# The last down pair of an MLP: kept product sums read back by plain transfers, and a second group of seven products

## The chip, the cores and the metric

The kernel runs on one core of one Trainium2 chip. The metric is the device time of one execution in microseconds, the median of repeated runs. Engine names are those of the profile: PE (matmul) with its weight loads PEld, DVE (vector), ACT (scalar), POOL (gpsimd), SP (the queue that issues most transfers).

## The reference

A decoder trunk of two layers on 256 tokens with 2048 features, in float32. Layer 0 has a dilated-window attention, layer 1 a block-sparse attention; the change touches neither. After its attention each layer runs an MLP with 8192 hidden features, and then a gate:

```python
hn = rmsnorm(h, mlp_norm_g[i])
h = h + jnp.square(jax.nn.relu(hn @ mlp_w1[i])) @ mlp_w2[i]
gate = jax.nn.sigmoid(rmsnorm(h, ple_norm_g[i]) @ ple_w_gate[i])
h = h + (p[i] @ ple_w_proj[i]) * gate
```

The first product is called "up" here, the second "down". Every product is done in three parts, because a float32 operand is split into a rounded high part and a low part: high times high, low times high, high times low.

## The kernel before, in words

**Chunks.** Weights arrive in chunks of 128 x 1024 floats (512 KB). For each chunk SP issues the load into a `raw` tile (5 buffers), ACT rounds it to `whi` (L252) and DVE subtracts to get `wlo` (L260). A plain chunk is 12 matmuls of 512 columns: two K-slices, two token halves, three parts. `Program.run` writes one order for all engines by hand: at chunk n it issues loads up to chunk n+7, `whi` up to n+4 and `wlo` up to n+3, then advances every pending piece of follow-up work by one step (each is a Python generator, and each `yield` is one step), and then issues the matmuls of chunk n. "Step n" below is this advance at chunk n. Each engine works through its own instructions strictly in that order.

**Blocks and pairs.** The MLP goes through the hidden features in four blocks b = 0 to 3 (`NFB` is 4). In each block the up products come as two pairs of column quarters, q = 0, 1 and q = 2, 3, and the down products likewise: pair (b, 0) makes the output quarters 0 and 1, pair (b, 2) the quarters 2 and 3. The order is: down (b, 0), up (b+1, 0), down (b, 2), up (b+1, 2). Block 3 ends with down pair (3, 0) and then two plain down quarters, `downs(3, 2)` and `downs(3, 3)`, which use `token_major` (8 plain chunks each, L598).

**Seven products instead of eight.** A pair goes through `pair_major` (L502). For chosen chunk positions c ("mixed") it multiplies a 2 x 2 arrangement of blocks with seven products instead of eight. Such a group takes the two weight chunks of the two quarters and makes two more on DVE (`make_t` L540, `make_u` L545 and L546), and needs sums of activation blocks ("forms"): tiles `xf` (4 buffers) for up, `hf` (2 buffers) for down. The group is issued as four program chunks of 6, 3, 6 and 6 matmuls, 21 where two plain chunks had 24. Some of its products are kept apart in PSUM banks P1, R6, Q5, Q7, and are turned into the result by four DVE operations on 128 x 512 each (`from_sums`, L882 to L885) before they are added to the rest. `mixed_down(b, q)` names the positions: (0, 4) for most down pairs, (0,) for pairs (0, 0) and (3, 0).

**Sums kept between blocks.** The running sums lie in DRAM: `y[q]` for each quarter, and `shared[q][0..1]` for the four kept banks of a pair. Blocks 0 to 2 add to them with accumulating transfers issued by POOL (`keep_sum`, L848). In block 3 the sums come back:

- `down_last(0)`, `sums`: ACT copies the four banks into two `y` row tiles (4 buffers, `row()`), POOL adds `shared[0]` onto them by two accumulating transfers (L930), DVE runs `from_sums`, POOL adds `y[0]`, `y[1]` by two accumulating transfers (L936).
- `down_last(0)`, `done(i)`: waits until `sums` has handed over its tiles, adds the banks of quarter i (L945), transposes on DVE (L709), writes the tile to a DRAM bounce tile `dU` (L206, SP) and reads it back in four transfers (L210, SP), adds it to the residual `x` (L726), and starts the next norm (`renorm`: ACT L357, L281; DVE L363, L289).
- `fetch(2)`, started after chunk 14 of the pair: two plain transfers bring `shared[2]` into two row tiles (L890), DVE runs `from_sums`, POOL adds `y[2]`, `y[3]` by two accumulating transfers (L896). The quarters 2 and 3 then add their matmul result onto these tiles (`down`, L856).

**Who else uses POOL and SP there.** The last up pair (3, 2) is still finishing while down pair (3, 0) runs: `up` transposes, and its bounce transfers go through POOL (L206 out, L210 back, four each), for quarter 2 at the pair's chunks 0 and 2, for quarter 3 at chunks 4 and 6; ACT and DVE then make the hidden tiles `h` (L778, L780), those of quarter 2 at step 7, those of quarter 3 at step 12. SP issues all weight loads.

Of the kernel before, what the change touches and what calls it, by code (L numbers as in the profile page):

```python
# [15 lines left out]
P = 128  # L16
D = 2048
T = 256
# [28 lines left out]


def mixed_down(b, q):
    return (0, 4) if (b, q) not in ((0, 0), (NFB - 1, 0)) else (0,)  # L50


def f32(ap):
# [117 lines left out]
def kernel(ctx: ExitStack, tc: tile.TileContext, a: dict, out: bass.AP):  # L171
# [566 lines left out]
    def mlp(layer, xg, norm, to, norm2, opening):  # L738
# [27 lines left out]
        def up(b, q, t, late=0):  # L766
            rest = REST[b > 0][q]

            nc.scalar.activation(t, t, AF.Square)
            for _ in range(2 + late):  # L770
                yield
            w = yield from turned(t, second if b == 0 and q == 1 else other if q % 2 else new, nc.gpsimd)
            for _ in range(rest):
                yield
            w4 = w.rearrange("p a (i j r) -> p a (i j) r", j=2, r=32)
            h = cur["z"].tile([P, 2, 4, T], F32R, tag="h", name="h", bufs=4)
            h5 = h.rearrange("p c i (j a r) -> p c a (i j) r", j=2, r=32)
            nc.scalar.copy(h5[:, 0], w4)  # L778
            yield
            nc.vector.tensor_sub(h5[:, 1], w4, f32(h5[:, 0]))  # L780
            for i in range(4):
                hid[b][4 * q + i] = (h[:, 0, i], h[:, 1, i])
            if q % 2 or (b == NFB - 1 and q):
                return

            a11, a21, a12, a22 = (w4[:, :, i] for i in range(4))
            nc.vector.tensor_sub(a22, a21, a22)
            nc.vector.tensor_sub(a21, a11, a21)
            nc.vector.tensor_sub(a11, a11, a22)
            nc.vector.tensor_sub(a12, a12, a11)  # L790
            yield
            f = cur["z"].tile([P, 2, 2 * T], F32R, tag="hf", name="hf", bufs=2)
            f5 = f.rearrange("p c (i a r) -> p c a i r", i=4, r=32)
            nc.scalar.copy(f5[:, 0], w4[:, :, :4])
            yield
            nc.vector.tensor_sub(f5[:, 1], w4[:, :, :4], f32(f5[:, 0]))
            turned_forms[b][2 * q] = f
# [83 lines left out]
        def from_sums(r, o):  # L881
# [2 lines left out]
            nc.vector.tensor_sub(r[:, 1], o[:, 1], r[:, 1])  # L884
            nc.vector.tensor_sub(o[:, 1], o[:, 0], o[:, 1])  # L885

        def fetch(q):
            rows = row(), row()
            for i in range(2):
                nc.gpsimd.dma_start(flat(rows[i]), shared[q][i])  # L890
            for _ in range(4):
                yield
            from_sums(*rows)
            yield
            for i in range(2):
                nc.gpsimd.dma_start(flat(rows[i]), y[q + i], accum_op=ALU.add)  # L896
                sums_so_far[q + i] = rows[i]

        def turning_tile(n):
            return f32(cur["z"].tile([P, 2, 2 * T], F32R, tag="hf", name="hf", bufs=2).rearrange("p c n -> p (c n)"))  # L900
# [20 lines left out]
        def down_last(q):  # L921
            ts = []

            def sums(aux):
                rows = row(), row()
                for t, names, kept in zip(rows, (("P1", "R6"), ("Q5", "Q7")), shared[q]):
                    for j, n in enumerate(names):
                        nc.scalar.copy(t[:, j], aux[n])
                    yield
                    nc.gpsimd.dma_start(flat(t), kept, accum_op=ALU.add)  # L930
                for _ in range(4):
                    yield
                from_sums(*rows)
                yield
                for i in range(2):
                    nc.gpsimd.dma_start(flat(rows[i]), y[q + i], accum_op=ALU.add)  # L936
                for _ in range(2):
                    yield
                ts.extend(rows)

            def done(i, ps):
                while not ts:
                    yield
                t = ts[i]
                nc.vector.tensor_add(t, ps, t)  # L945
                yield
                w = yield from turned(t, turning_tile if i else new, steps=3)
                add_turned(q + i, w)
                yield
                yield from in_pairs(normed, q + i)  # L950

            return sums, done

        def down_mixed(b, q):
            sums, done = down_kept(b, q) if b < NFB - 1 else down_last(q)
            m = mixed_down(b, q)
            if (b, q) == (0, 0):
                order = [(i, c) for i in range(2) for c in (1, 2, 3)] + [(0,)] + [(i, c) for c in (4, 5) for i in range(2)]
            else:
                order = [(0, c) for c in (1, 2, 3)] + [(0,)] + [(1, c) for c in (1, 2, 3)]  # L960
                order += [(0, 5), (1, 5), (4,)] if len(m) == 2 else [(i, c) for c in (4, 5) for i in range(2)]
            order += [(i, c) for i in range(2) for c in (6, 7)]
            pair_major(lambda i, c: a["w2"][layer * 128 + (b * 4 + q + i) * 8 + c], order, hid[b], turned_forms[b], sums, done,
                       {(0, 0): {13: [lambda: all_forms(MIXED[3:])]}, (NFB - 1, 0): {14: [lambda: fetch(2)]}}.get((b, q)), (3, 1, 0, 2))

        up_mixed(0, 2)
        for b in range(NFB):
# [1034 lines left out]
```

## Time and profile before

| | |
|---|---|
| median of 3 runs | 2426.03 us (2425.81 to 2428.92) |
| the profiled execution | 2427.97 us, its span 2426.2 us |
| granted PE clock, mean | 0.998 |
| PE busy | 2405.9 us, 99% of the span |
| DVE, ACT, POOL busy | 1987.6, 1480.0, 147.6 us |
| transfers | 565.85 MB, 233 GB/s mean |

The span is the time between the first and the last instruction; the execution is 1.8 us longer. Times in the views count from the start of the span. In a list of instructions a bracket gives the idle time of the engine before the instruction and what ended it. In a table of stretches, PE (x) counts the instructions that touch the stretch, PEclk is the granted clock as a share of full speed, and the DMA share is the mean busy share of 16 engines.

### The profile page before, as it was taken

The page shows a single profiled execution, that of the slowest core. Times are in us where ns is not written, and L with a number is a line of the kernel's source. Part 1 is how long each engine was busy: PE and PEld are TensorE (multiplying, and loading weights), DVE is VectorE, ACT ScalarE, POOL GpSimd, SP SyncE. Part 2 cuts the span into 40 slices and gives each one's busy share as a digit, 9 for nine tenths or more (in the row PEclk, how much of TensorE's full clock was granted, in tenths as well). Part 3 has the DMA queues.
Part 4 walks back from the last instruction along what each step waited for, and adds up shares of the span by engine and source line. Part 5 has one row for each costly group of instructions (what it writes and reads, how often), then busy time and mean ns, then how long its engine had stood idle before and what let it go on. Part 6 is the DMA issues. An engine that isn't in the chain of part 4 may idle for free.

```text
span 2426.2 us, 33519 instructions
## 1 busy us (share of the span) xinstructions
PE 2405.9 (99%) x11613; PEld 2023.3 (83%) x11613; DVE 1987.6 (82%) x2960; ACT 1480.0 (61%) x2161; POOL 147.6 (6%) x246
## 2 busy tenths in 40 slices
PE   9999999999999999999999999999999999999998
PEld 8888888888888888887788889988888888888787
DVE  7867687688898988886777989867898898888676
ACT  6544444567566666664664788756666666666456
POOL 0000000001001100111000000000100100111000
PEclk9999999999999999999999999999999999999999
DMA  8666666778778788879886753476777878888985
GB/s 282 204 216 213 199 208 193 223 216 270 245 248 260 247 255 258 249 250 284 257 247 209 256 176 120 131 226 218 254 239 260 260 252 252 258 246 259 286 254 151
DMA packets 171882, 565.85 MB, mean 233 GB/s; under 512 B 20608, under 2 KB 36416, under 8 KB 171712
## 3 DMA queue, kind: packets, MB, share of 16 engines
q1 hardware_dynamic: 150672, 494.73, 63.4%
q0 software_dynamic: 20464, 68.19, 11.0%
q8 instruction: 91, 1.49, 0.3%
q10 hardware_dynamic: 576, 0.79, 0.1%
q14 instruction: 79, 0.65, 0.1%
HBM read 504.39 MB, written 59.24 MB: 232 GB/s over the span
## 4 chain that ended last, share of the span: by engine, by line
PE 90%; issue 4%; DMA 4%; DVE 1%; POOL 0%; ACT 0%; SPq 0%; ACTq 0%; DVEq 0%; POOLq 0%
PE at L502 33%; PE at L598 13%; PE mm L393 11%; PE mm L598 11%; PE mm L502 8%; PE mm L395 6%; PE at L393 1%; DMA dU<-z 1%; DMA y<-s 1%; DMA raw<-in_w 1%; PE at L395 1%; DVE wlo L260 1%; PE at L1824 1%; DMA w<-dU 0%; PE mm L1848 0%
## 5 line engine op out<-in xcount | busy, mean ns | idle before, releaser
L260 DVE TENSOR_TENSOR wlo<-raw,whi 128x1024 fp32r<-128x1024 f32 (+1 forms) x953 | 1094.9, 1171 | 252.7 <-ACT whi L252 85.0
L252 ACT CAST whi<-raw 128x1024 fp32r<-128x1024 f32 (+1 forms) x953 | 939.2, 1013 | 451.8 <-DMA raw<-in_w 133.4
L502 PE MATMUL at<-whi,h 128*128 128x512 f32 x1504 | 463.3, 389 | 0.4 <-DVE h L780 0.4
L393 PE MATMUL mm<-xa,whi 128*128 128x512 f32 x1104 | 372.4, 396 | 0.0
L502 PE MATMUL at<-whi,xa 128*128 128x512 f32 x1144 | 352.1, 389 | 0.0
L502 PEld LDWEIGHTS at<-whi,h 128*128 128x128 f32 x1504 | 282.3, 188 | 59.5 <-DVE h L780 0.8
L502 PE MATMUL at<-wlo,h 128*128 128x512 f32 x752 | 292.7, 389 | 0.4 <-DVE wlo L260 0.4
L395 PE MATMUL mm<-xa,wlo 128*128 128x256 f32 x1104 | 274.2, 278 | 0.0
L502 PEld LDWEIGHTS at<-whi,xa 128*128 128x128 f32 x1144 | 214.7, 188 | 44.5
L502 PE MATMUL at<-wlo,xa 128*128 128x512 f32 x572 | 222.5, 389 | 0.0
L395 PEld LDWEIGHTS mm<-xa,wlo 128*128 128x128 f32 x1104 | 207.3, 188 | 17.7
L393 PEld LDWEIGHTS mm<-xa,whi 128*128 128x128 f32 x1104 | 193.5, 188 | 31.0 <-issue 0.4
L598 PE MATMUL at<-whi,xa 128*128 128x512 f32 x672 | 208.1, 391 | 0.1
L598 PE MATMUL mm<-whi,xa 128*128 128x512 f32 x656 | 202.7, 390 | 0.0
L502 PEld LDWEIGHTS at<-wlo,h 128*128 128x128 f32 x752 | 141.1, 188 | 30.0 <-DVE wlo L260 0.8
L252 ACT CAST whi<-ts 128x1024 fp32r<-128x1024 f32 x78 | 82.0, 1051 | 123.0 <-DVE ts L540 122.1
L598 PEld LDWEIGHTS at<-whi,xa 128*128 128x128 f32 x672 | 124.8, 188 | 26.3 <-ACT whi L252 0.8
L598 PEld LDWEIGHTS mm<-whi,xa 128*128 128x128 f32 x656 | 122.5, 188 | 25.0
L598 PE MATMUL at<-wlo,xa 128*128 128x512 f32 x336 | 130.9, 391 | 0.2 <-DVE wlo L260 0.2
L598 PE MATMUL mm<-wlo,xa 128*128 128x512 f32 x328 | 127.7, 389 | 0.0
L502 PEld LDWEIGHTS at<-wlo,xa 128*128 128x128 f32 x572 | 107.4, 188 | 22.4
L260 DVE TENSOR_TENSOR wlo<-ts,whi 128x1024 fp32r<-128x1024 f32 x78 | 95.1, 1220 | 8.8 <-PE at L502 4.5
(445 smaller groups left out, 3377.9 us busy)
## 6 DMA issues: line engine op xcount, KB each, us to landing
raw<-in_w SPq DMA_DIRECT2D x512, 512.0 KB, 5.2
raw<-in_w_qk SPq DMA_DIRECT2D x96, 512.0 KB, 4.2
raw<-in_w_gate SPq DMA_DIRECT2D x64, 512.0 KB, 4.8
raw<-in_w_kv SPq DMA_DIRECT2D x48, 512.0 KB, 4.4
raw<-in_w_v SPq DMA_DIRECT2D x47, 512.0 KB, 4.5
y<-y POOLq DMA_DIRECT2D x32, 512.0 KB, 9.2
raw<-in_w_q SPq DMA_DIRECT2D x32, 512.0 KB, 4.4
raw<-in_w_oB SPq DMA_DIRECT2D x32, 512.0 KB, 3.7
```

Source lines behind the costliest of these rows:

```text
L252: nc.scalar.copy(hi[:, c], t[:, c])
L260: nc.vector.tensor_sub(lo[:, c], t[:, c], f32(hi)[:, c])
L393: nc.tensor.matmul(ps, hi[:, col:col + P], rhs, start=first, stop=False)
L395: nc.tensor.matmul(ps[:, :T], lo[:, col:col + P], rhs[:, :T], start=False, stop=last)
L502: nc.tensor.matmul(ps, x_, w_, start=b not in touched, stop=end and last[b] == n and i == 2)
L598: nc.tensor.matmul(st[j], *parts[j][i], start=k == i == 0, stop=k == kt - 1 and i == 2)
L1824: nc.tensor.transpose(tr[:, i * P:(i + 1) * P], src, ident)
```

## The change

Four things change, all of them in block 3 of both layers' MLPs.

1. `mixed_down(3, 0)` becomes (0, 4): two plain chunks of down pair (3, 0) become a second group of seven products. The pair then has the order that pairs (1, 0) to (2, 2) have: 20 program chunks instead of 18, 186 matmuls instead of 189, with the four kept banks complete after chunk 15 and not after chunk 6. `up` now also makes forms `hf` for quarter 2 of block 3 (four small DVE operations, one ACT cast, one DVE subtraction).
2. The kept sums are read by plain transfers into `xf` tiles, which nothing else uses after the last up pair: `fetch_shared(0)` after chunk 1, `fetch_shared(2)` after chunk 14. In `sums`, DVE adds each of the four banks onto these tiles; the four ACT copies and the two accumulating transfers L930 are gone.
3. For quarters 2 and 3, `fetch` reads `y[2]` and `y[3]` by plain transfers into row tiles, and `finish_sums(2)` runs `from_sums` and two DVE additions of 128 x 1024 in place of the two accumulating transfers L896.
4. `done(0)` and `done(1)` wait for `sums`, which now ends at step 23 (it ended at step 16), so both begin there. The two accumulating transfers of `y[0]`, `y[1]` stay.

```diff
 def mixed_down(b, q):
-    return (0, 4) if (b, q) not in ((0, 0), (NFB - 1, 0)) else (0,)
+    return (0, 4) if b or q else (0,)
...
-            if q % 2 or (b == NFB - 1 and q):
+            if q % 2:
                 return
...
+        kept = {}
+
+        def fetch_shared(q):
+
+            kept[q] = [cur["z"].tile([P, 2, 2 * T], F32R, tag="xf", name="xf", bufs=len(MIXED)) for _ in range(2)]
+            kept[q] = [f32(t) for t in kept[q]]
+            for i in range(2):
+                nc.gpsimd.dma_start(kept[q][i], shared[q][i])
+
         def fetch(q):
-            rows = row(), row()
+            sums_so_far[q] = row()
+            nc.gpsimd.dma_start(flat(sums_so_far[q]), y[q])
+
+        def with_y(q, i):
+            nc.vector.tensor_add(kept[q][i], kept[q][i], sums_so_far[q + i])
+            sums_so_far[q + i] = kept[q][i]
+
+        def finish_sums(q):
+            for _ in range(6):
+                yield
+            from_sums(*kept[q])
             for i in range(2):
-                nc.gpsimd.dma_start(flat(rows[i]), shared[q][i])
-            for _ in range(4):
-                yield
-            from_sums(*rows)
-            yield
-            for i in range(2):
-                nc.gpsimd.dma_start(flat(rows[i]), y[q + i], accum_op=ALU.add)
-                sums_so_far[q + i] = rows[i]
+                for _ in range(2):
+                    yield
+                with_y(q, i)
...
             def sums(aux):
-                rows = row(), row()
-                for t, names, kept in zip(rows, (("P1", "R6"), ("Q5", "Q7")), shared[q]):
+                for t, names in zip(kept[q], (("P1", "R6"), ("Q5", "Q7"))):
                     for j, n in enumerate(names):
-                        nc.scalar.copy(t[:, j], aux[n])
+                        nc.vector.tensor_add(t[:, j], aux[n], t[:, j])
                     yield
-                    nc.gpsimd.dma_start(flat(t), kept, accum_op=ALU.add)
+                from_sums(*kept[q])
+                yield
+                for i in range(2):
+                    nc.gpsimd.dma_start(kept[q][i], y[q + i], accum_op=ALU.add)
                 for _ in range(4):
                     yield
-                from_sums(*rows)
-                yield
-                for i in range(2):
-                    nc.gpsimd.dma_start(flat(rows[i]), y[q + i], accum_op=ALU.add)
-                for _ in range(2):
-                    yield
-                ts.extend(rows)
+                ts.extend(kept[q])
...
-                order = [(0, c) for c in (1, 2, 3)] + [(0,)] + [(1, c) for c in (1, 2, 3)]
-                order += [(0, 5), (1, 5), (4,)] if len(m) == 2 else [(i, c) for c in (4, 5) for i in range(2)]
+                order = [(0, c) for c in (1, 2, 3)] + [(0,)] + [(1, c) for c in (1, 2, 3)] + [(0, 5), (1, 5), (4,)]
             order += [(i, c) for i in range(2) for c in (6, 7)]
...
-                       {(0, 0): {13: [lambda: all_forms(MIXED[3:])]}, (NFB - 1, 0): {14: [lambda: fetch(2)]}}.get((b, q)), (3, 1, 0, 2))
+                       {(0, 0): {13: [lambda: all_forms(MIXED[3:])]}, (NFB - 1, 0): {1: [lambda: fetch_shared(0)], 
+                                         14: [lambda: fetch_shared(2)],
+                                         15: [lambda: fetch(2), lambda: fetch(3), lambda: finish_sums(2)]}}.get((b, q)), (3, 1, 0, 2))
```

## The prediction

> **What bounds the kernel.** I read the page first, then a table of stretches cut at the first matmul of each stage around the change.
>
> ```profile
> PE 2405.9 (99%) x11613; PEld 2023.3 (83%) x11613; DVE 1987.6 (82%) x2960; ACT 1480.0 (61%) x2161; POOL 147.6 (6%) x246
> ```
> ```profile
> 975.95:1018.11 42.16, 42.16 (x188) 34.91 (x187) 37.17 (x41) 26.66 (x33) 8.18 (x13) 1.00 0.78 240
> 1058.91:1102.49 43.58, 43.19 (x190) 35.32 (x189) 31.39 (x30) 26.07 (x30) 10.27 (x16) 1.00 0.86 255
> 1102.49:1151.58 49.09, 44.45 (x193) 35.80 (x192) 36.06 (x46) 21.15 (x31) 4.39 (x8) 1.00 0.98 292
> 2223.66:2266.49 42.83, 42.83 (x190) 35.47 (x189) 32.38 (x31) 24.95 (x28) 10.26 (x16) 1.00 0.88 260
> 2266.49:2315.18 48.69, 45.44 (x193) 37.10 (x192) 34.95 (x46) 22.10 (x32) 1.80 (x2) 0.96 0.94 288
> ```
> ```profile
> 1157.19 5.44 PE mm L598 x24
> ```
>
> PE sets the time: only fewer matmuls or fewer stalls of PE help. The rows are, in order: down pair (2, 2) of layer 0, which already has two groups of seven; down pair (3, 0) of layer 0; the 16 plain chunks behind it; and the latter two in layer 1. The first number is the length. From the chain of waits, 24 matmuls take 5.44 us, 0.2267 us each, so a plain chunk takes 2.72 us and 16 of them 43.52 us. They take 49.09 and 48.69 us: 5.57 and 5.17 us are lost right behind the pair, 10.74 us in all. Pair (2, 2) loses nothing: 186 x 0.2267 = 42.16. So I looked for the cause of the loss, in the instructions of PE and then of DVE.
>
> ```profile
> 1116.72 0.50 PE L598 MATMUL mm<-wlo,h 128*128 128x512 f32 x1 [2.73 <-DVE wlo L260]
> 1140.03 0.50 PE L598 MATMUL at<-wlo,h 128*128 128x512 f32 x1 [1.21 <-DVE wlo L260]
> 1143.75 0.50 PE L598 MATMUL at<-wlo,h 128*128 128x512 f32 x1 [0.70 <-DVE wlo L260]
> 2281.24 0.50 PE L598 MATMUL mm<-wlo,h 128*128 128x512 f32 x1 [3.25 <-DVE wlo L260]
> ```
> ```profile
> 1109.63 0.69 DVE L882 TENSOR_TENSOR y<-y 128x512 f32<-128x512 f32 x1 [2.02 <-DMA y<-s]
> 1112.25 0.69 DVE L883 TENSOR_TENSOR y<-y 128x512 f32<-128x512 f32 x1 [1.93 <-DMA y<-s]
> ...
> 1130.48 1.29 DVE L726 TENSOR_TENSOR x<-w,x 128x512 f32<-128x512 f32 x2 [3.52 <-DMA w<-dU]
> ```
> ```profile
> 2272.95 0.69 DVE L882 TENSOR_TENSOR y<-y 128x512 f32<-128x512 f32 x1 [2.94 <-DMA y<-s]
> 2276.78 0.69 DVE L883 TENSOR_TENSOR y<-y 128x512 f32<-128x512 f32 x1 [3.13 <-DMA y<-s]
> ...
> 2278.84 1.22 DVE L945 TENSOR_TENSOR y<-at,y 128x1024 f32<-128x1024 f32 x1
> 2279.97 1.21 DVE L260 TENSOR_TENSOR wlo<-raw,whi 128x1024 fp32r<-128x1024 f32 x1
> ```
>
> PE waits for `wlo`, which stands on DVE behind `from_sums` of quarters 2 and 3, and that waits for the transfers `y<-s` of `fetch(2)`: 3.95 us in layer 0, 6.07 in layer 1. After the first stall DVE has no lead left, and the next wait (L726, 3.52 us) reaches PE again at 1140 and 1143. In layer 1 the stall costs more than its 3.25 us:
>
> ```profile
> 2280.97:2283.69 2.72, 2.45 (x8) 1.97 (x9) 2.72 (x4) 0.74 (x1) 0.00 (x0) 0.74 1.01 194
> 2283.69:2286.41 2.72, 2.72 (x10) 2.13 (x9) 2.72 (x3) 0.00 (x0) 0.00 (x0) 0.64 1.06 247
> ```
>
> The granted clock falls to 0.74 and 0.64. At those clocks 0.26 x 2.72 + 0.36 x 2.72 = 1.7 us more go.
>
> Why are those loads late? POOL issues them behind the accumulating transfers L936, which wait for `from_sums` of quarters 0 and 1, and they land some 12 us later.
>
> ```profile
> 1072.03 0.56 POOL L206 DMA_DIRECT2D dU<-z  x1 [0.68 <-DVE z L709]
> 1078.33 2.19 POOL L210 DMA_DIRECT2D y<-dU  x4 [5.74 <-DMA dU<-z]
> 1080.51 2.01 POOL L930 DMA_DIRECT2D y<-s  x2
> 1097.54 1.75 POOL L936 DMA_DIRECT2D y<-y  x2 [15.02 <-DVE y L884]
> 1098.80 1.58 POOL L890 DMA_DIRECT2D y<-s  x2
> ```
>
> The transfer queues in 1083 to 1093 us, with the accumulating transfers L930 in the software queue, and then in 1107 to 1110, with plain `y<-s` in it:
>
> ```profile
> q0 software_dynamic: 405, 1.35, 67.2%
> q1 hardware_dynamic: 357, 1.29, 37.2%
> ```
> ```profile
> q0 software_dynamic: 168, 0.62, 50.6%
> ```
>
> Accumulating: 67.2% of 10 us for 1.35 MB is 5.0 us per MB of all 16 engines. Plain: 50.6% of 3 us for 0.62 MB is 2.4. A 512 KB transfer thus takes 2.6 us or 1.3 us.
>
> **The change, part by part.**
>
> *Second group of seven.* Pair (3, 0) gets the form of pair (2, 2). Three matmuls fewer are 0.68 us per layer; with the 0.74 us that layer 0 loses inside the pair, 43.58 and 42.83 become 42.16: -1.42 and -0.67, in sum -2.1 us. The added work on DVE (`make_t`, `make_u`, forms) is what pair (2, 2) does in its 37.17 busy us, hidden under 42.16 us of PE. If that cover fails, the most that comes back is this gain.
>
> *fetch_shared(0)* moves ahead of the bounce of the last up pair: on POOL it passes the four L210 of quarter 2 and all of quarter 3. Two issues cost about 2 us of POOL (L930: 2.01), inside the wait for `dU<-z` to land (5.74 idle for quarter 3). Nothing is late.
>
> *fetch_shared(2), fetch(2), fetch(3)* are in POOL's order behind L210 of quarter 3 and ahead of the y accumulates, and wait for no engine that is still busy. They should go out at about 1080.5, where L930 goes today, more than 20 us before DVE needs them. Four plain transfers take 5.2 us of the engines, as the two accumulating ones now (2 x 2.6). Altogether six accumulating and two plain transfers (18.2 us) become two and six (13.0 us), two of them in a slack stretch. The 7.9 us less in the busy stretch I cost at nothing, since it only keeps weights early.
>
> [...]
>
> *Sums on DVE.* Per layer DVE takes four bank additions (0.69 each by L882), two additions of 1.22 (L945); ACT loses four copies. Steps 16 to 25: ten subtractions at 1.13 (row distance of L945 to the next rows), four additions 2.8, two `from_sums` 5.6, two y additions and two `done` additions 4.9, two transposes 2.4: 27.0 us against 27.2 us of PE. DVE starts that stretch about three chunks ahead (8 us), and neither `from_sums` waits any more: quarter 2's has its data since about 1090, quarter 0's needs only SBUF and PSUM. The y accumulates go out at step 19 for use at step 23, 10.9 us, against 5.4 us that the first of them takes in the chain now. If they are late, the `done` additions wait, and subtraction 27 stands behind them.
>
> ```profile
> 1097.54 5.37 DMA y<-y
> ```
>
>  So the losses of 5.57 and 5.17 go: -10.7 us. Bounds: 0 (all come back) and -10.7.
>
> *Quarter 3's hidden tiles.* They are needed at chunk 16, which now begins 42.16 - 4 x 2.72 = 31.3 us into the pair, at 1090.2 or a little later. Subtraction 16 is behind them on DVE.
>
> ```profile
> 1088.34 1.05 ACT L778 CAST h<-y 128x1024 fp32r<-128x1024 f32 x1 [3.38 <-DMA y<-dU]
> ```
> ```profile
> 1089.42 1.23 DVE L780 TENSOR_TENSOR h<-y,h 128x1024 fp32r<-128x1024 f32 x1 [3.20 <-ACT h L778]
> ```
>
> That ends at 1090.65, the subtraction at 1091.8: 0 to 1.2 us of stall per layer. I take 0.6 for both layers together, as both numbers end within a microsecond of the need.
>
> *Quarters 0 and 1 finish together.* Both additions move to step 23, both bounces on SP to steps 25 and 28, both `x` additions to step 31. That is five and three chunks later against the plain chunks.
>
> ```profile
> 1119.63 2.01 SPq L210 DMA_DIRECT2D w<-dU  x4
> ...
> 1125.84 3.62 SPq L210 DMA_DIRECT2D hf<-dU  x4
> ```
> ```profile
> 1133.96 0.88 DVE L363 SCALAR_TENSOR_TENSOR xa<-x,gains,xa 128x256 fp32r<-128x256 f32 x2
> 1134.75 0.42 DVE L289 TENSOR_TENSOR acc<-acc,sq 128x256 f32<-128x256 f32 x1
> 1136.35 1.29 DVE L726 TENSOR_TENSOR x<-hf,x 128x512 f32<-128x512 f32 x2 [1.18 <-DMA hf<-dU]
> 1137.56 1.28 DVE L856 TENSOR_TENSOR y<-mm,y 128x512 f32<-128x512 f32 x2
> ```
>
> L726 stood 10.85 and 10.51 us behind its read-back. On SP eight read-backs now stand in a row, with the loads of chunks 36 and later behind them. Steps 28 to 37 on DVE: ten subtractions 11.3, three `x` additions 3.9, L856 1.3, one transpose 1.2, twelve rounds of L363 and L289 at 0.8 make 9.6: 27.3 us of work for 27.2 us of PE, plus the wait for the read-backs. Laid out in order, DVE reaches step 31 about four chunks ahead of PE and waits some 7 us for the second read-back; its lead is about nil near chunk 38. A new stall of 0 to 6 us per layer is possible there. I take 1.5, near the lower end, as layer 0's second stall today (1.21 + 0.70) began without lead too.
>
> Sum against the profiled execution of 2427.97 us: -2.1 - 10.7 + 0.6 + 3.0 = -9.2, giving 2418.8. The median of the runs is 1.94 us lower, so on it 2426.03 - 9.2 = 2416.8.
>
> **The rivals.**
>
> *Half comes back.* The fetch stall goes, but the crowd at steps 31 to 37 costs 4 to 5 us per layer. For it: the sum of 27.3 leaves no room, and the eight read-backs queue on SP. Against: only weights and bounces move then. -2.1 - 10.7 + 0.6 + 9 = -3.2: 2422.8.
>
> *Slower.* Place: SP's eight read-backs in a row. If `dU` lands 3 us later and the read-backs take the 10.85 us of today one behind the other, DVE resumes about 6.3 us later than I laid out, and the loads behind them too. Quarter 2's bounce wants the same single `w` tile and stands behind as well. It decides from the point where the second `x` addition starts later than chunk 35. Price per layer 1.5 + 6.3 us, and 1.7 us each for the clock as in layer 1's stall: 2 x 9.5 = 19.0, less the same gains, +0.6 + 19.0 - 12.8 = +6.8: 2432.8. Against it: those stretches hold no accumulating transfer any more. [...]
>
> *It doesn't do what it says.* The loads don't go out early, because POOL holds them until some older tile is free, and `from_sums` waits as it does now. Against: the `xf` readers end with the up pair. Then only the matmuls are won, -1.4 to -2.1: 2424.3.
>
> **How the numbers follow.** The forecast gets 0.63, half back 0.17, no early loads 0.09, slower 0.11. The forecast's own band is 2413 (all 12.8 us) to 2420.5. The range reaches through the half case to 2424, which leaves out slower and most of the no-early-loads case, under 0.2. A difference of 0.2%, 4.85 us, is about what the measurement can tell, so faster is below 2421.2: 0.61 of the forecast and 0.07 of the half case give 0.68; slower 0.11; the rest, 0.21, is the same.
>
> **What would show it.** Right: pair (3, 0) takes 42.2 us; `y<-s` loads near 1063 and 1080; no idle of DVE before L882 and L883; the 16 plain chunks in 44 to 46 us; granted clock 1.00 there in layer 1. Wrong: idle before `from_sums`, L945 waiting for `y<-y`, a stall at chunk 16 above 1.2 us, or PE waiting for `wlo` between chunks 35 and 41 for more than 3 us.

## The result, and the profile after

The changed kernel takes 2414.11 us (median; 2412.49 to 2414.96), the kernel before 2425.98 us beside it. The ratio is 0.9947, with a 95% interval of 0.993 to 0.9965: faster by 0.35 to 0.7%. The profiled execution went from 2427.97 to 2413.51 us, its span from 2426.2 to 2411.7: 14.5 us less. Forecast were 2416.8 us and a difference of 9.2 us. The profiled execution before lies 2.0 us above its median and the one after 0.6 us below, so the 14.5 us that the views account for are 11.9 us on the medians.

The page's busy row, after:

```profile
PE 2401.1 (100%) x11607; PEld 2021.2 (84%) x11607; DVE 2009.7 (83%) x2992; ACT 1481.4 (61%) x2159; POOL 144.3 (6%) x246
```

PE has six instructions fewer and DVE 22.1 us more work, which cost nothing as a whole. Where the time went shows in the table of stretches, cut as in the prediction: down pair (3, 0) and the 16 plain chunks of layer 0, then of layer 1.

```profile
1059.34:1102.10 42.76, 42.46 (x187) 34.84 (x186) 38.57 (x43) 25.85 (x29) 8.72 (x16) 1.00 0.93 316
1102.10:1145.62 43.52, 43.52 (x193) 36.04 (x192) 40.47 (x53) 22.17 (x34) 4.46 (x8) 1.00 0.94 292
2214.69:2257.50 42.81, 42.49 (x187) 34.83 (x186) 38.22 (x43) 25.66 (x28) 8.72 (x16) 1.00 0.94 312
2257.50:2301.02 43.52, 43.52 (x193) 36.04 (x192) 41.61 (x53) 23.06 (x37) 1.80 (x2) 1.00 0.95 300
```

Both plain stretches take 43.52 us, 192 matmuls at 0.2267 us and nothing else, at a granted clock of 1.00 in both layers (0.96 in layer 1 before). The bookkeeping over the whole span, each length the distance between the first matmuls of two stages:

| stretch, us | before | after | difference | forecast |
|---|---|---|---|---|
| up to pair (3, 0), layer 0 | 1058.91 | 1059.34 | +0.43 | 0 |
| pair (3, 0), both layers | 86.41 | 85.57 | -0.84 | -2.1 + 0.6 |
| 16 plain chunks, both layers | 97.78 | 87.04 | -10.74 | -10.7 + 3.0 |
| from layer 0's plain chunks to layer 1's pair | 1072.08 | 1069.07 | -3.01 | 0 |
| from layer 1's plain chunks to the end | 111.02 | 110.68 | -0.34 | 0 |

The waits of PE in the whole execution (total us, times, longest):

```profile
PE mm L1241 <- DVE ones L222: 1.1, 1, 1.1
PE at L502 <- DVE wlo L260: 0.6, 2, 0.3
PE at L598 <- ACT whi L252: 0.3, 1, 0.3
PE at L598 <- DVE wlo L260: 0.2, 1, 0.2
```

Of the stall of 2.73 us at 1116 and of those at 1140, 1143 and 2281, nothing is left. The two waits at L502 are subtraction 16, once per layer. In the list of PE's instructions, the one of layer 0:

```profile
1091.53 0.50 PE L502 MATMUL at<-wlo,h 128*128 128x512 f32 x1 [0.30 <-DVE wlo L260]
```

The list of POOL's instructions shows the six plain loads where the prediction put them, near 1063 and 1080, and one pair of accumulating transfers (L946) where three pairs were (L930, L936, L896):

```profile
1063.10 1.07 POOL L894 DMA_DIRECT2D xf<-s  x2 [0.26 <-issue]
...
1080.94 1.10 POOL L894 DMA_DIRECT2D xf<-s  x2
1082.03 1.05 POOL L898 DMA_DIRECT2D y<-y  x2
1102.77 1.80 POOL L946 DMA_DIRECT2D xf<-y  x2 [19.70 <-DVE xf L884]
```

The list of DVE's instructions: neither `from_sums` has an idle time in front of it (2.02 and 1.93 us before), the hand-over's additions (L955) find `y[0]` and `y[1]` landed, and the two additions to `x` wait 1.09 and 0.79 us, where 3.52 and 1.18 were and some 7 were laid out.

```profile
1100.33 0.69 DVE L882 TENSOR_TENSOR xf<-xf 128x512 f32<-128x512 f32 x1
...
1106.52 0.69 DVE L882 TENSOR_TENSOR xf<-xf 128x512 f32<-128x512 f32 x1
...
1112.70 2.35 DVE L955 TENSOR_TENSOR xf<-at,xf 128x1024 f32<-128x1024 f32 x2
...
1131.87 1.29 DVE L726 TENSOR_TENSOR x<-w,x 128x512 f32<-128x512 f32 x2 [1.09 <-DMA w<-dU]
1133.96 1.29 DVE L726 TENSOR_TENSOR x<-hf,x 128x512 f32<-128x512 f32 x2 [0.79 <-DMA hf<-dU]
```

*The 3 us that no term of the forecast holds.* They lie in the gate behind layer 0's plain chunks. There PE sums the squares for the next norm in one short product with a vector of ones ("the norm column", L298), and needs all four quarters of `x`. The last quarter's result is taken from its bank by L856, goes through the bounce, and comes back as the last L726. Those three instructions before, and then after (lists of DVE's and PE's instructions, in order of time):

```profile
1159.56 1.28 DVE L856 TENSOR_TENSOR y<-at,y 128x512 f32<-128x512 f32 x2
1176.19 1.30 DVE L726 TENSOR_TENSOR x<-w,x 128x512 f32<-128x512 f32 x2 [5.96 <-DMA w<-dU]
1183.88 0.61 PE L298 MATMUL mm<-ones,acc 128*128 128x1 f32 x4 [1.93 <-DVE acc L289]
```
```profile
1149.31 1.28 DVE L856 TENSOR_TENSOR xf<-at,xf 128x512 f32<-128x512 f32 x2
1165.95 1.30 DVE L726 TENSOR_TENSOR x<-w,x 128x512 f32<-128x512 f32 x2 [5.25 <-DMA w<-dU]
1175.54 0.50 PE L298 MATMUL mm<-ones,acc 128*128 128x1 f32 x4
```

Before, the column came 7.69 us behind L726 and PE had waited for it. After, it came 29.92 us behind the end of the plain chunks (1145.62), which is PE's own pace, and L726 was 9.59 us ahead. By that pace the column was due at 1151.58 + 29.92 = 1181.50 before, and was 2.38 us late. Quarter 3's L856 stood 7.98 us behind the end of the plain chunks then, and stands 3.69 behind it now.

### The profile page after: what moved, and what is told of

It reads as the page before. It is cut to its first block, busy times and chain, and to the rows that moved or that the text cites. A ratio compares the mean times of both kernels' runs of the same rounds, so it can differ in the third digit from the quotient of the medians.

```text
span 2411.7 us, 33518 instructions
## 1 busy us (share of the span) xinstructions
PE 2401.1 (100%) x11607; PEld 2021.2 (84%) x11607; DVE 2009.7 (83%) x2992; ACT 1481.4 (61%) x2159; POOL 144.3 (6%) x246
## 4 chain that ended last, share of the span: by engine, by line
PE 91%; issue 4%; DMA 2%; DVE 1%; ACT 1%; POOL 0%; SPq 0%; ACTq 0%; DVEq 0%; POOLq 0%
PE at L502 33%; PE at L598 14%; PE mm L598 13%; PE mm L393 11%; PE mm L502 7%; PE mm L395 6%; PE at L393 1%; PE at L395 1%; DVE wlo L260 1%; DMA w<-dU 1%; PE at L1835 1%; DMA raw<-in_w 0%; DMA dU<-z 0%; PE mm L1859 0%; PE mm L1598 0%
## 5 line engine op out<-in xcount | busy, mean ns | idle before, releaser
L502 PE MATMUL at<-whi,h 128*128 128x512 f32 x1480 | 455.9, 389 | 0.0
L502 PE MATMUL at<-whi,xa 128*128 128x512 f32 x1144 | 352.2, 389 | 0.0
L502 PEld LDWEIGHTS at<-whi,h 128*128 128x128 f32 x1480 | 277.8, 188 | 57.9 <-DVE h L780 0.3
L502 PE MATMUL at<-wlo,h 128*128 128x512 f32 x740 | 288.4, 390 | 0.6 <-DVE wlo L260 0.6
L502 PEld LDWEIGHTS at<-whi,xa 128*128 128x128 f32 x1144 | 214.7, 188 | 44.5
L502 PE MATMUL at<-wlo,xa 128*128 128x512 f32 x572 | 222.5, 389 | 0.0
L502 PEld LDWEIGHTS at<-wlo,h 128*128 128x128 f32 x740 | 138.9, 188 | 30.9 <-DVE wlo L260 2.2
L502 PEld LDWEIGHTS at<-wlo,xa 128*128 128x128 f32 x572 | 107.4, 188 | 22.3
```

The lines of the kernel that those rows point to most:

```text
L502: nc.tensor.matmul(ps, x_, w_, start=b not in touched, stop=end and last[b] == n and i == 2)
```

## The experiments

The theories were these. *Place*: what counts is that the kept sums are issued early on POOL, ahead of everything that waits for DVE. *Amount*: what counts is how many accumulating transfers run in the busy stretch. *Crowd*: quarters 0 and 1 finishing together cost something at steps 28 to 37, and more if they come later. And the second group of seven is worth its matmuls or not. Each ratio is against runs of the kernel before taken beside it (medians 2425.29 to 2426.23 us); each view is of one execution.

### The second group of seven alone

To the kernel before:

```diff
-    return (0, 4) if (b, q) not in ((0, 0), (NFB - 1, 0)) else (0,)
+    return (0, 4) if b or q else (0,)
-            if q % 2 or (b == NFB - 1 and q):
+            if q % 2:
-     (NFB - 1, 0): {14: [lambda: fetch(2)]}
+     (NFB - 1, 0): {16: [lambda: fetch(2)]}
```

> The kernel before with the second group of seven and its forms, all six accumulating transfers kept; fetch(2) still starts two chunks before the pair's end, which here is ahead of L930 and L936 in POOL's order. Theory A (the loss came from loads of quarters 2 and 3 that went out late on POOL): the pair takes 42.2 to 43 us, DVE does not wait for y<-s before the second from_sums, the 16 plain chunks take 44 to 47 us, total 8 to 12 us under before. Theory B (the loss came from accumulating transfers, which fill the transfer engines): the 16 plain chunks still take 48 to 50 us, total 0 to 3 us under before. Theory C (the second group of seven itself, by moving the work of quarters 0 and 1 later, made the gain): total 10 to 13 us under before.

Measured: 2437.33 us, ratio 1.0046 (1.0031 to 1.0061): slower by 11 us, where all three theories had it faster. Its pair takes 42.16 us and its plain chunks 43.52 in both layers, so nothing is lost there. The loss lies behind them, 8.6 us in layer 0 and 8.1 in layer 1 against the kernel before. DVE's and PE's instructions in the gate:

```profile
1178.95 1.29 DVE L726 TENSOR_TENSOR x<-w,x 128x512 f32<-128x512 f32 x2 [7.55 <-DMA w<-dU]
1186.63 0.61 PE L298 MATMUL mm<-ones,acc 128*128 128x1 f32 x4 [2.07 <-DVE acc L289]
```

With four banks complete only after chunk 15 and two rounds of accumulating transfers behind them, the hand-over comes at step 25. Quarter 3's L856 is 15.3 us behind the end of the plain chunks (1145.42), and the column 7.68 us behind L726, 11.3 late. So the group with the old transfers costs more than it saves: it needs the rest of the change. `fetch(2)` also goes out ahead of the accumulating transfers of `y[0]` and `y[1]` here, so two things changed, not the group by itself.

### The plain loads alone

The changed kernel with one group of seven in pair (3, 0):

```diff
-    return (0, 4) if b or q else (0,)
+    return (0, 4) if (b, q) not in ((0, 0), (NFB - 1, 0)) else (0,)
-            if q % 2:
+            if q % 2 or (b == NFB - 1 and q):
```

> The changed kernel with one group of seven in pair (3, 0), as before; loads and sums as in the change. Theories A and B: the 16 plain chunks take 43.5 to 45 us in both layers, the pair 42.8 to 43.6, total 9 to 12.5 us under before. Theory C: the 16 plain chunks take 48 us or more and the total is 0 to 3 us under before.

Measured: 2415.03 us, ratio 0.9957 (0.994 to 0.9973), 0.9 us above the full change, which the two intervals can't tell apart. The plain loads are nearly the whole gain, and the plain chunks take 43.52 us in both layers. The pair, from the table of stretches:

```profile
1060.00:1102.84 42.84, 42.84 (x191) 35.47 (x189) 33.72 (x35) 20.92 (x23) 10.60 (x18) 1.00 0.96 294
```

42.84 against 42.76 with the second group: three matmuls less are 0.68 us, and the stall at chunk 16 takes most of it back. That stall isn't in every trace: the same pair takes 42.16 us in both layers in two kernels further down (no accumulating transfer, two groups in every pair).

With one group the kept banks are complete earlier, so POOL issues L946 earlier too, and here the loads for quarters 2 and 3 stand behind it:

```profile
1086.42 1.85 POOL L946 DMA_DIRECT2D xf<-y  x2 [4.48 <-DVE xf L884]
1087.72 1.66 POOL L894 DMA_DIRECT2D xf<-s  x2
1088.80 1.63 POOL L898 DMA_DIRECT2D y<-y  x2
```
```profile
1113.33 0.69 DVE L882 TENSOR_TENSOR xf<-xf 128x512 f32<-128x512 f32 x1
```

Nothing waits for them: they go out some 25 us before `from_sums` of these quarters.

### Only POOL's order

The kernel before, with `fetch(2)` one chunk earlier, so that its loads pass the accumulating transfers of `y[0]` and `y[1]` on POOL; a `yield` keeps its `from_sums` at its step:

```diff
-            for _ in range(4):
+            for _ in range(5):
                 yield
             from_sums(*rows)
-     (NFB - 1, 0): {14: [lambda: fetch(2)]}
+     (NFB - 1, 0): {13: [lambda: fetch(2)]}
```

> The kernel before with one thing moved: fetch(2) starts after chunk 13 and not 14, so that its two loads stand ahead of the y accumulates L936 in POOL's order; from_sums and what follows stay at their steps. All six accumulating transfers stay. Theory A: no DVE wait for y<-s before the second from_sums, the 16 plain chunks take 43.5 to 46 us, total 7 to 11 us under before. Theory B: the waits move elsewhere, the 16 plain chunks take 47 us or more, total 0 to 3 us under before.

Measured: 2427.71 us, ratio 1.0007 (0.9997 to 1.0016): no difference; the 7 to 11 us of theory A didn't come. POOL, DVE and PE:

```profile
1079.64 0.86 POOL L890 DMA_DIRECT2D y<-s  x1
1088.07 0.55 POOL L890 DMA_DIRECT2D y<-s  x1 [7.57 <-DVE h L780]
```
```profile
1102.37 1.23 DVE L945 TENSOR_TENSOR y<-at,y 128x1024 f32<-128x1024 f32 x1 [3.79 <-DMA y<-y]
...
1106.91 0.68 DVE L882 TENSOR_TENSOR y<-y 128x512 f32<-128x512 f32 x1
...
1127.07 1.29 DVE L726 TENSOR_TENSOR x<-w,x 128x512 f32<-128x512 f32 x2 [3.60 <-DMA w<-dU]
```
```profile
1136.93 0.50 PE L598 MATMUL at<-wlo,h 128*128 128x512 f32 x1 [1.64 <-DVE wlo L260]
```

The loads go out 19 and 11 us earlier (the second after a wait, since its row tile is read by L780 until then), no idle is left before L882, and the stall of 2.73 us is gone. But L945 now waits 3.79 us for `y[0]`, L726 still waits 3.60, and the second stall stays: 1.64 us, and 0.71 at 1140.65, where 1.21 + 0.70 were. The prediction called the second stall an echo of the first one. It has a cause of its own. It is not the accumulated sums of quarters 0 and 1, for it goes where these are kept and only quarters 2 and 3 change (two kernels down). What the traces of layer 0 put in its place are the accumulating transfers L896 of quarters 2 and 3, which POOL issues at 1109.34 here (1113.97 before), just as quarters 0 and 1 bounce.

### The plain loads issued late

The changed kernel, with the four loads for quarters 2 and 3 after chunk 19, behind L946 on POOL:

```diff
-     14: [lambda: fetch_shared(2)],
-     15: [lambda: fetch(2), lambda: fetch(3), lambda: finish_sums(2)]}
+     15: [lambda: finish_sums(2)],
+     19: [lambda: fetch_shared(2), lambda: fetch(2), lambda: fetch(3)]}
```

> The changed kernel with the four plain loads for quarters 2 and 3 issued after chunk 19, so that they stand behind the y accumulates of quarters 0 and 1 on POOL; nothing else is moved. Theory A: DVE waits some 5 to 7 us before the second from_sums, of which DVE's lead hides a part, and PE loses 1 to 4 us per layer in the 16 plain chunks; total 2 to 8 us above the changed kernel. Theory B: as the changed kernel within 1.5 us.

Measured: 2432.9 us, ratio 1.0027 (1.0015 to 1.0038), 18.8 us above the changed kernel, where theory A had 2 to 8. DVE, then PE in both layers:

```profile
1114.78 0.69 DVE L882 TENSOR_TENSOR xf<-xf 128x512 f32<-128x512 f32 x1 [8.85 <-DMA xf<-s]
```
```profile
1120.74 0.50 PE L598 MATMUL mm<-wlo,h 128*128 128x512 f32 x1 [3.45 <-DVE wlo L260]
...
2288.27 0.79 PE L598 MATMUL mm<-wlo,h 128*128 128x512 f32 x1 [4.31 <-DVE wlo L260]
```

Plain transfers of the same number and size bring nothing when they go out late: L946 goes out at 1102.10, these loads from 1103.39 on, and DVE is at `from_sums` 2.5 us later. Time is what counts, and not the place behind L946 as such, which they also have in the kernel with plain loads alone. The kernel with only the order moved showed that being early isn't enough.

### Half the quarters each

Both start from the kernel with plain loads alone. One gives quarters 2 and 3 back their old `fetch(2)`, with the accumulating transfers and its place on POOL:

```diff
-     (NFB - 1, 0): {1: [lambda: fetch_shared(0)],
-                    14: [lambda: fetch_shared(2)],
-                    15: [lambda: fetch(2), lambda: fetch(3), lambda: finish_sums(2)]}
+     (NFB - 1, 0): {1: [lambda: fetch_shared(0)], 14: [lambda: fetch(2)]}
```

> The kernel before (one group of seven in the pair) with the change's loads and sums for quarters 0 and 1 alone: fetch_shared(0) by plain transfers, bank sums on DVE. fetch(2) stays as before, after chunk 14, with its accumulating y transfers. Theory D (the chain is L930: the first from_sums waits for these accumulating transfers, L936 waits for from_sums, and the loads for quarters 2 and 3 stand behind L936 on POOL): the first from_sums does not wait, L936 goes out near 1086 us, the loads behind it near 1088, the second from_sums does not wait; the 16 plain chunks take 43.5 to 45.5 us, total 8 to 12 us under before. Theory B (what counts is how many accumulating transfers are left, here four of six): total 2 to 5 us under before.

The other gives quarters 0 and 1 back their old `sums`:

```diff
-                        nc.vector.tensor_add(t[:, j], aux[n], t[:, j])
+                        nc.scalar.copy(t[:, j], aux[n])
...
+                    nc.gpsimd.dma_start(flat(t), back, accum_op=ALU.add)
-     1: [lambda: fetch_shared(0)],
```

> The kernel before with the change's plain loads and DVE additions for quarters 2 and 3 alone; quarters 0 and 1 keep the ACT copies and the accumulating transfers L930 and L936. Theory D: DVE still waits about 3 us before the first from_sums, L936 goes out near 1097, the four loads behind it; DVE waits again before the second from_sums or at the y additions, and the 16 plain chunks take 46 to 49 us, total 2 to 6 us under before. Theory B (four of six accumulating transfers left): the same as the run with quarters 0 and 1 alone within 2 us.

Measured: 2425.4 us, ratio 0.9999 (0.9985 to 1.0012), for the change on quarters 0 and 1 alone; 2420.76 us, 0.998 (0.9966 to 0.9993), for quarters 2 and 3 alone. Neither half brings half of 11: one brings nothing, where theory D had 8 to 12 us, and the other 4.5, where it had 2 to 6. Each leaves four accumulating transfers, and so does a changed kernel further down that takes 2414.65 us, so the amount doesn't decide. In the first of them the plain chunks do win (45.79 and 44.73 us), and the gate gives it back. POOL there, then DVE and PE:

```profile
1108.06 1.79 POOL L905 DMA_DIRECT2D y<-y  x2 [19.96 <-DVE y L884]
```
```profile
1126.01 1.30 DVE L726 TENSOR_TENSOR x<-w,x 128x512 f32<-128x512 f32 x2 [4.09 <-DMA w<-dU]
...
1180.36 0.61 PE L298 MATMUL mm<-ones,acc 128*128 128x1 f32 x4 [2.37 <-DVE acc L289]
```

The accumulating transfers of quarters 2 and 3 run while quarters 0 and 1 bounce; L726 waits 4.09 us, and the last quarter is late for the column.

With quarters 2 and 3 alone the plain chunks of layer 0, and DVE behind them:

```profile
1102.50:1146.02 43.52, 43.52 (x193) 36.04 (x192) 35.81 (x46) 22.26 (x32) 2.55 (x6) 1.00 0.99 327
```
```profile
1122.14 1.29 DVE L726 TENSOR_TENSOR x<-w,x 128x512 f32<-128x512 f32 x2 [1.94 <-DMA w<-dU]
```

Both stalls of layer 0 are gone, although `y[0]` and `y[1]` are still accumulated and the loads for quarters 2 and 3 still stand behind them on POOL (1096 us). Layer 1 takes 44.94 us. In this kernel `from_sums` of quarters 2 and 3 also comes 4 us later against the plain chunks than before, which gives the loads time; no run takes that apart from the kind of transfer. The profiled execution (2418.08 us) is 2.7 us under its median, so its views show less loss than is typical of this kernel.

### Accumulating `y`, in the changed kernel

Quarters 2 and 3 take `y[2]`, `y[3]` by accumulating transfers again, in the second kernel `y[0]`, `y[1]` come by plain ones too, so that none is left:

```diff
-                with_y(q, i)
+                nc.gpsimd.dma_start(kept[q][i], y[q + i], accum_op=ALU.add)
...
-     15: [lambda: fetch(2), lambda: fetch(3), lambda: finish_sums(2)]
+     15: [lambda: finish_sums(2)]
```

> The changed kernel with y[2], y[3] added by two accumulating transfers after the second from_sums, as before, in place of plain loads and two DVE additions. Theory D: nobody waits for them before step 28, total within 2 us of the changed kernel. Theory B: two accumulating transfers more fill the engines while the read-backs of quarters 0 and 1 are due, total 3 to 6 us above the changed kernel.

```diff
-                    nc.gpsimd.dma_start(kept[q][i], y[q + i], accum_op=ALU.add)
-                for _ in range(4):
+                    with_y(q, i)
                     yield
-     15: [lambda: fetch(2), ...
+     15: [lambda: fetch(0), lambda: fetch(1), lambda: fetch(2), ...
```

> The changed kernel without its last two accumulating transfers: y[0] and y[1] are loaded by plain transfers too, and DVE adds them; the hand-over of quarters 0 and 1 then comes at step 21 and not 23. Theory lead (PE stalls only where DVE's lead over it is used up): the two additions cost DVE 2.4 us where its lead is 3.7 us or more, and the earlier hand-over gives it back; 2414 us, within 1.5 of the changed kernel, plain chunks 43.52. Theory transfers (each accumulating transfer in this stretch costs time by itself): 1 to 3 us under the changed kernel, 2411 to 2413. Theory crowd (DVE has no room in steps 16 to 25, 27.0 us of work for 27.2): 2.4 us more there show as a stall, 2416 to 2419.

Measured: 2414.65 us with four accumulating transfers (ratio 0.995, 0.9931 to 0.9969), 2416.12 with none (0.9965, 0.9951 to 0.9979). Neither can be told from the changed kernel's 0.9947; none is better. Without any, two more plain loads join the four in a row near 1081, the last at 1089.30 us, only when L780 has left its row tile; ACT waits 2.90 us for a weight chunk at 1098, and layer 0's plain chunks take 44.71 us.

### The hand-over one and two steps later

```diff
-                for _ in range(4):
+                for _ in range(6):
                     yield
                 ts.extend(kept[q])
```

> The changed kernel with sums handing over quarters 0 and 1 two steps later, at step 25 and not 23, no transfer changed. It asks why the run with the second group alone lost 16 us behind the plain chunks. If the late finish itself is the cause (eight read-backs, and quarter 2's read-back behind them for the single w tile): PE waits in the gate for xa and for L856, 4 to 12 us above the changed kernel. If its waits of 7 us for accumulating y transfers at L945 were the cause: 0 to 2 us above the changed kernel.

With `range(5)` it is one step:

> The changed kernel with the hand-over of quarters 0 and 1 one step later (step 24, between 23 of the change and 25, which took 2425.2 us). A slope (each step costs by its own lateness): 5.5 us above the changed kernel, 2419.6. An edge behind step 24 (the stall begins only when the second addition to x comes too late): 2414 to 2416. An edge at once: 2425. PE's waits, if any, stand behind the 16 plain chunks, in the gate, and not in them.

Measured: 2425.19 us two steps later (ratio 0.9998, 0.9985 to 1.0011), 2420.17 one step later (0.998, 0.9969 to 0.9991). From 2414.11 that is +11.1 and +6.1 us: some 5.5 us a step, as the slope in the second expectation had it, and two steps eat the whole gain. The plain chunks still take 43.52 us in both layers of both kernels; nearly all is lost behind. The traces show no even slope there: one and two steps cost 2.1 and 5.7 us behind layer 0's plain chunks, but 3.9 in both cases behind layer 1's. DVE and PE in layer 0, one step later:

```profile
1169.85 1.29 DVE L726 TENSOR_TENSOR x<-w,x 128x512 f32<-128x512 f32 x2 [5.31 <-DMA w<-dU]
1177.53 0.61 PE L298 MATMUL mm<-ones,acc 128*128 128x1 f32 x4 [1.31 <-DVE acc L289]
```

The kernel with the second group alone also hands over at step 25, and is still 12.1 us above the one two steps later. So the late hand-over is about half of what it loses against the changed kernel. In its list of DVE's instructions L945 waits 4.61 and 2.63 us for accumulated sums besides; how the other half divides isn't shown.

L856, L726 and L298 of the last quarter give one rule that holds in both layers of all fourteen kernels. The column runs at the later of two times: 29.92 us behind the end of the plain chunks, or 7.68 us behind quarter 3's L726. The last column is measured apart from it, as the stretch from layer 0's plain chunks to layer 1's pair. Layer 0, in us:

| kernel | end of plain chunks | quarter 3's L856 behind it | column late by | stretch, over 1069.07 |
|---|---|---|---|---|
| changed | 1145.62 | 3.69 | 0 | 0 |
| quarters 2 and 3 alone | 1146.02 | 6.45 | 0 | -0.08 |
| two groups in every pair | 1145.53 | 2.90 | 0 | 0.74 |
| plain loads alone | 1146.36 | 5.04 | 0 | 0.77 |
| four accumulating transfers | 1146.12 | 6.86 | 0.90 | 1.28 |
| two groups, no accumulating transfer | 1146.63 | 6.56 | 1.48 | 2.27 |
| no accumulating transfer | 1145.70 | 6.52 | 1.63 | 2.30 |
| only POOL's order | 1148.51 | 7.82 | 1.10 | 1.09 |
| one step later | 1145.84 | 8.01 | 1.77 | 2.13 |
| before | 1151.58 | 7.98 | 2.38 | 3.01 |
| quarters 0 and 1 alone | 1147.69 | 7.94 | 2.75 | 4.81 |
| late loads | 1151.97 | 8.91 | 3.61 | 5.60 |
| two steps later | 1146.80 | 12.51 | 5.63 | 5.66 |
| second group alone | 1145.42 | 15.30 | 11.29 | 11.58 |

Where the stretch is 2.0 us longer than the column is late (late loads, quarters 0 and 1 alone), the granted clock is 0.50 for 3.4 us behind the column, which costs 1.7 us.

L856 of quarter 3 stands in DVE's order behind the norm rounds (L363, L289) of quarters 0, 1 and 2, and those behind the read-backs. Whatever delays the read-backs delays the last quarter, and PE pays for it some 30 us later, where the plain chunks look untouched.

### A second group in every pair

The changed kernel, with two groups also in pair (0, 0); and the same together with the kernel that has no accumulating transfer:

```diff
-    return (0, 4) if b or q else (0,)
+    return (0, 4)
-                order = ... + [(0,)] + [(i, c) for c in (4, 5) for i in range(2)]
+                order = ... + [(0,), (0, 5), (1, 5), (4,)]
```

> The changed kernel, and the very first down pair of each layer (block 0, pair 0) gets two groups of seven too: 3 matmuls fewer per layer, 3 x 0.2267 = 0.68 us. If matmuls saved in a down pair come through: the profile shows that pair 0.68 us shorter and the time is 1.4 us lower, 2412.7. If DVE's forms take the place of the matmuls (its lead there is used up): no gain, 2414, or up to 3 us more, with PE waiting for DVE in that pair.

> No accumulating transfer in the last block and two groups of seven in every down pair (the two edits of this job's first two kernels together). If both effects stand by themselves: 2414.1 - 1.4 + (0 to -1.5) = 2411.2 to 2412.7. If the saved matmuls are taken back by DVE in the first pair: 2413 to 2414.

Measured: 2415.56 us (ratio 0.9952, 0.9938 to 0.9967) and 2415.81 us (0.9959, 0.9944 to 0.9974): no gain, neither beats the changed kernel, and the second lies above both sums that were forecast for it. Pair (0, 0) of layer 0 in the changed kernel, and then here, with the first of PE's two waits in it (the other is 0.49 us, at 593.70):

```profile
560.42:603.29 42.87, 42.87 (x190) 35.43 (x189) 36.15 (x43) 30.32 (x38) 7.11 (x13) 1.00 0.87 284
```
```profile
560.35:604.25 43.90, 43.02 (x187) 34.68 (x186) 39.11 (x47) 30.61 (x39) 7.11 (x13) 1.00 0.79 237
```
```profile
590.14 0.50 PE L502 MATMUL mm<-wlo,hf 128*128 128x512 f32 x1 [0.38 <-DVE wlo L260]
```

Three matmuls fewer, and the pair is 1.03 us longer, because DVE has 2.96 us more to do there and PE waits for `wlo`.

## Why the prediction was right, point by point

*The loss in the plain chunks goes* (-10.7): right, and to the full, -10.74. The steps shown: loads near 1063 and 1080, no idle before `from_sums`, clock 1.00. For the first stall the mechanism was right: with the loads late it comes back. The reason given for the second stall, that it came from the first, fell with the order-only kernel, where the first goes and the second stays. In layer 0 it stays in the three kernels whose accumulating transfers of `y[2]`, `y[3]` run as quarters 0 and 1 bounce (before, only POOL's order, quarters 0 and 1 alone), and is gone with quarters 2 and 3 alone. Layer 1 has no second stall before, though these transfers run there too, so they aren't the whole cause; what else it needs stays open. The term thus has its full size in part for a reason that the working didn't have, and that part was luck.

*Second group of seven* (-2.1) and *quarter 3's hidden tiles* (+0.6): the lengths of the pair give -0.84 together, where -1.5 were forecast. The stall stood where it was put, at chunk 16. Its size was off: 42.76 and 42.81 are 0.60 and 0.65 us above 42.16, 1.25 for both layers, twice the term, though each is inside the range of 0 to 1.2 a layer. Traces of other kernels have this pair at 42.16, so the size changes from one trace to the next.

*The four plain loads in a row* (costed at nothing): right for PE. In the whole execution it waited 0.3 us for `whi`, so the weights kept up. The price was low, though: from 1081 to 1092 us the software queue took 73.6% of the engines for 2.33 MB, 3.5 us per MB where 2.4 were counted.

*Quarters 0 and 1 finish together* (+3.0): this is the step that failed. The working had DVE waiting some 7 us for the second read-back and left without lead near chunk 38. Measured are waits of 1.09 and 0.79 us, and no stall; counted on from the stall at chunk 16, the subtraction for chunk 38 ends some 4 us before PE starts that chunk. The twelve norm rounds and the ten subtractions came as counted; what was wrong is the wait. L726 follows its read-back by 8.2 and 8.4 us, where 10.85 and 10.51 were taken over from a stretch with accumulating transfers in it. That is about half of the 5 us too many; the prediction gives no times from which to place the rest. SP's list, after:

```profile
1123.69 1.75 SPq L210 DMA_DIRECT2D w<-dU  x4
1125.54 4.92 SPq L210 DMA_DIRECT2D hf<-dU  x4
```

For the first read-back the accumulating transfers fit as the cause: 10.9 to 12.3 us in layer 0 of the three kernels that have them just ahead of it, at most 9.7 in the others. For the second they don't suffice: with plain loads alone it takes 11.5 us and no accumulating transfer is near. That stays open.

*What no step had*: the account ended at chunk 41, and so it missed the norm column. Its 2.38 us of lateness in layer 0 went, most of the 3.01 us there. The missed gain of 3.0 and the crowd of +3.0 that didn't come, less the 0.7 us by which the pair fell short, make up the 5.3 us between 9.2 and 14.5. On the medians the gain is 11.9 us, and the forecast only 2.7 us off; how much of that is the column can't be read from one trace.

*The rivals.* "Half comes back" didn't happen. "Slower" named the right place, the late finish of quarters 0 and 1 (that the single `w` tile is what binds was not tested), but the change stays on the safe side of it, by less than one step: the kernels one and two steps later lose 6.1 and 11.1 us. "It doesn't do what it says" was priced too low. With late loads the kernel isn't at 2424.3 but at 2432.9, because stalls of 3.45 and 4.31 us come with a granted clock of 0.50 for 3.41 and 6.81 us, and the last quarter is late as well.

## What to carry to other kernels

In a kernel whose engines each follow a fixed order, ask for each transfer how long before its reader it goes out, and not only how many bytes it moves: with the same four loads the kernel was 11.9 us faster than before when they went out early on POOL, and 6.7 slower when they went out late. What a transfer stands behind mattered through that time: behind L946, loads that went out 25 us before `from_sums` kept nobody waiting, and later ones held it for 8.85 us. Ask too what else moves while a bounce is on its way (read-back to L726: 10.85 us before, 8.2 after). When a finish is moved, follow its chain to the last consumer. A chain that is late for a norm 30 us on doesn't show in the stretch that was changed: with the hand-over one step later the plain chunks took 43.52 us, and the column came 1.77 us late. And ask whether the engine that feeds a saved matmul has lead to spare: in pair (0, 0) three matmuls fewer came with 1.03 us more, as DVE had 2.96 us more to do.

## What the runs showed of the hardware

*The clock after a stall.* The prediction's 0.74 and 0.64 are means over stretches of 2.72 us. Cut finer, the granted clock is 1.00 or 0.50 in the stretches shown here. Those at 0.50 behind the 3.25 us of the kernel before, behind the 3.45 and 4.31 us of the late loads, and behind a wait of 1.59 us for the norm column in layer 1 (hand-over one step later):

```profile
2282.28:2285.69 3.41, 3.41 (x9) 2.65 (x8) 3.41 (x5) 0.00 (x0) 0.00 (x0) 0.50 1.06 227
...
1122.02:1125.43 3.41, 3.41 (x10) 2.65 (x9) 3.41 (x4) 1.04 (x1) 0.00 (x0) 0.50 0.83 291
...
2285.98:2292.79 6.81, 4.52 (x11) 3.56 (x12) 6.78 (x8) 1.26 (x2) 0.00 (x0) 0.50 0.48 147
...
2337.55:2340.95 3.40, 3.40 (x9) 2.61 (x9) 2.73 (x4) 0.92 (x2) 0.00 (x0) 0.50 0.80 257
```

They last 3.41, 3.41, 6.81 and 3.40 us. They need not begin with the stall's end: before, PE was back for 1.0 us, and with the 4.31 us the clock fell while PE was still idle, 2.3 us before its next matmul. The length of the stall doesn't decide it either: the clock was 0.50 behind a wait of 1.59 us, and the 2.73 us of the kernel before left it at 1.00:

```profile
1116.72:1122.00 5.28, 5.28 (x23) 4.35 (x24) 5.28 (x5) 0.59 (x1) 0.00 (x0) 1.00 1.04 216
```

*Accumulating transfers.* With two, four or none of them in the changed kernel, the times are 2414.11, 2414.65 and 2416.12 us. They did take more of the engines than the plain loads. The software queue of the changed kernel, from 1103 to 1112 us with L946 in it, and from 1081 to 1092 with the four plain loads (2.10 MB of the 2.33):

```profile
q0 software_dynamic: 285, 1.04, 65.2%
```
```profile
q0 software_dynamic: 679, 2.33, 73.6%
```

That is 5.6 us per MB against 3.5, with weight loads beside both. In this order the difference costs no time that the runs can tell. Where they run as quarters 0 and 1 bounce, layer 0 has the second stall (1.21 and 0.70 us before, 1.64 and 0.71 with only POOL's order).
